# Other start addresses for the split weights, and a strided layout in the first MLP matrix, in a fp32 decoder layer

## The chip, the cores and the metric

The kernel runs on one core of one Trainium2 chip. The metric is the device time of one execution in microseconds (us); lower is better. The times before come from three runs, and one further execution was taken with the hardware profiler.

## What is computed

One layer of a decoder trunk on 512 tokens of width 2048, all in float32. Cut to what matters:

```python
h = rmsnorm(x, g_mix)
z = h @ w_in                                  # 2048 -> 10248 columns
cb, cc, cv, q, k, v, f_logit, gate_c, gate_a = split(z)
conv_branch = (cb * causal_dwconv(cc * cv, conv_w)) @ w_conv_out
attn_branch = forgetting_attention(q, k, v, log_sigmoid(f_logit + b_f)) @ w_attn_out
merged = sigmoid(gate_c + b) * conv_branch + sigmoid(gate_a + b) * attn_branch
x = x + merged @ w_mix_out
h = rmsnorm(x, g_mlp)
u = square(relu(h @ w_ff1))                   # 2048 -> 8192
x = x + u @ w_ff2                             # 8192 -> 2048
return rmsnorm(x, g_final)
```

## The kernel before

Every product of float32 matrices is made of three matmuls in a rounded format (fp32r). Each operand is split into a high part (a rounded copy) and a low part (the rest), and high times high, high times low and low times high are added in PSUM. The helper `split` does this for weights: ScalarE copies the block `src` with rounding into a tile `th` (line 101), and VectorE subtracts that from `src` into a tile `tl` (line 102). `parts` hands out a pair of such tiles from two buffers of each; its argument `at` is the element at which the data begin inside the buffer.

The two large matrices that are multiplied with the normed input, `w_in` and `w_ff1`, go through the class `Group`. A group takes two blocks of columns and both halves of the rows of the weight, and multiplies them by a scheme in the manner of Strassen and Winograd: seven products instead of eight. The seven sums of activation quarters are kept split in the tiles `A11`, `A12`, `A22`, `S1` to `S4`; the sums and differences of weight quarters are made by VectorE in place (line 105, `sub`) in the four load buffers `x0` to `x3`. `head` does the two products `A11` and `A12`, `tail` the other five. Each product is one call of `run`, which asks `parts` for `th` and `tl`, calls `split`, and then calls the group's matmul routine.

- `mm_cols` (lines 136, 138 and 140) is used where the result is wanted with the columns on the partitions: queries and keys (4 groups), the convolution's inputs (6), the gates (8), all from `w_in`, and the whole of `w_ff1` (16 groups). The quarter of the weight is 128 rows by 8 blocks by 256 columns. One stationary operand is 128 columns of one block of `th` or `tl`; the moving operand is 256 tokens of an activation quarter. A run has 48 matmuls: for each of 8 blocks and of 2 halves `j` of the 256 columns one with `th` and the activations' high part (line 136), one with `th` and their low part (138), and then all 16 with `tl` (140). Before, half `j` is 128 neighbouring columns.
- `mm_rows` (lines 154, 156 and 158) has the roles exchanged: the activations are stationary and `th` and `tl` are moving. It is used by the two groups of attention values, `gV1` (260 columns wide) and `gV0` (256), and with 512 columns by the second MLP matrix `w_ff2`, whose seven products are in `unit`.

The constants `WBUF` (2112 elements, the length of one buffer), `SHIFT` and `PAD` (16 elements each) set where data lie. With them every 256-wide group begins 16 elements, 64 bytes, into its buffer; the 260-wide one begins at its start.

Around the change the order is set by the program text: the two products of a head, the attention heads between key/query groups, then the convolution groups, the gates, the branch outputs and `w_mix_out` (`gemm_t` and `gemm_n`, 512 columns, with tiles of their own from `parts`), the first MLP matrix, where the heads of four groups go ahead and the other twelve groups follow whole, and the second. Weights are loaded by SyncE's queue (line 178), one block of 1024 KB each, as soon as one of the four buffers is free. Results of the first MLP matrix are squared, summed and split on ScalarE and VectorE (`put_u`, tiles `r` and `rh`) and written to memory by GpSimd's queue (`s_d`).

Of the kernel before, what the change touches and what calls it, by code (L numbers as in the profile page):

```python
# [15 lines left out]
P = 128  # L16
S = 512
D = 2048
KT = D // P
NT = S // P  # L20
HS = S // 2
# [13 lines left out]
VW = AW // 4  # L35
V1W = (AW // 2 + NH) // 2
QSCALE = float(P) ** -0.5
WBUF, SHIFT, PAD = 33 * 64, 16, 16


ORDER = ("A11", "A12", "S4", "S2", "S3", "S1", "A22")
# [4 lines left out]
def tile_hybrid_block(ctx: ExitStack, tc, x, g_mix, w_in, b_f, b_gate, conv_w, w_conv_out,  # L46
                      w_attn_out, w_mix_out, g_mlp, w_ff1, w_ff2, g_final, out):
    nc = tc.nc
    x, out = x[0], out[0]
    w_in, w_conv_out, w_attn_out, w_mix_out = w_in[0], w_conv_out[0], w_attn_out[0], w_mix_out[0]  # L50
    w_ff1, w_ff2 = w_ff1[0], w_ff2[0]
# [48 lines left out]
    def split(src, hi, lo):  # L100
        nc.scalar.activation(out=hi, in_=src, func=AF.Copy)  # L101
        nc.vector.tensor_tensor(out=lo, in0=src, in1=hi.bitcast(F32), op=ALU.subtract)  # L102

    def sub(out, a, b):
        nc.vector.tensor_tensor(out=out, in0=a, in1=b, op=ALU.subtract)  # L105

    def add(out, a, b):
        nc.vector.tensor_tensor(out=out, in0=a, in1=b, op=ALU.add)  # L108

    def parts(shape, at=0):  # L110

        q, w = shape[1:]
        return tuple(main.tile([P, WBUF], F32R, tag=tag, name=tag, bufs=2)[:, at:at + q * w]
                     .rearrange("p (q c) -> p q c", q=q) for tag in ("th", "tl"))
# [12 lines left out]
    def mm_cols(ps, Sx, hi, lo, first):  # L127

        ps = ps[0].rearrange("p (j s) -> p j s", j=2)
        nq = hi.shape[1]  # L130
        for part in range(2):
            for q in range(nq):
                for j in range(2):
                    o, js = ps[:, j, :], slice(j * P, (j + 1) * P)
                    if part == 0:
                        nc.tensor.matmul(o, hi[:, q, js], Sx[:, 0, q, :], start=first and q == 0 and j == 0, stop=False,  # L136
                                         skip_group_check=True)
                        nc.tensor.matmul(o, hi[:, q, js], Sx[:, 1, q, :], start=False, stop=False, skip_group_check=True)  # L138
                    else:
                        nc.tensor.matmul(o, lo[:, q, js], Sx[:, 0, q, :], start=False, stop=q == nq - 1,  # L140
                                         skip_group_check=True)

    def mm_rows(ps, Sx, hi, lo, first):
# [15 lines left out]
                                         skip_group_check=True)  # L159


    free, later = [0, 1, 2, 3], []

    class Group:

        def __init__(self, view, c1, c2, w, ST, mm, banks, put, scale=1.0):
            self.view, self.cs, self.w, self.ST, self.mm, self.banks = view, (c1, c2), w, ST, mm, banks
            self.put, self.scale, self.at = put, scale, {}  # L170

        def load(self, i, j):

# [8 lines left out]
            return [bank(i, which) for i in self.banks["abcd".index(which)]]  # L182

        def run(self, ps, n, src, first):
            hi, lo = parts([P, KT // 2, self.w], SHIFT if self.w == HS else 0)
            split(src, hi, lo)
            self.mm(ps, self.ST[n], hi, lo, first)

        def snap(self, ps, scale=1.0):
            s = otile([P, 2, self.w], "o")  # L190
# [192 lines left out]
    for t in range(NT):  # L383
        h = xp[t // 2][:, t % 2]
        n = 4 if t == 0 else 2
# [52 lines left out]
    def kq(hp, banks):  # L438
        return Group(w_in, COL_K + hp * HS, COL_Q + hp * HS, HS, Q1.ST, mm_cols, banks, store_kq(hp), QSCALE)
# [16 lines left out]
    def at(name, shape=None, dt=F32):  # L456
        return pb.tile(shape or [P, S], dt, tag="at", name=name, bufs=6)
# [33 lines left out]
    c1 = at("c1", [NH, S])  # L491
# [5 lines left out]
    c2 = at("c2", [NH, S])  # L497
# [80 lines left out]
    n = NH // 2  # L578
    for g in (4, 2, 0, 5, 3, 1):
        def put_z(i, j, v, g=g):  # L580
            f = 4 * (g % 2) + 2 * j
            nc.sync.dma_start(out=z_d[g // 2, f:f + 2, :, i * HS:(i + 1) * HS].rearrange("b p c -> p b c"), in_=v)

        whole(Group(w_in, g * S, g * S + HS, HS, Q1.ST, mm_cols, steady(n), put_z))
        n += 1
        if g < 2:
            for f in range(4 * g, 4 * g + 4):
                conv_job(f)

    for f in range(0, KT, 2):  # L590
        def put_g(i, j, v, f=f):
            for b in range(2):
                k = j * KT + f + b
                nc.scalar.activation(out=v[:, b, :], in_=v[:, b, :], func=AF.Sigmoid, bias=bgT[:, k:k + 1])
            nc.sync.dma_start(out=g_d[j, f:f + 2, :, i * HS:(i + 1) * HS].rearrange("b p c -> p b c"), in_=v)

        whole(Group(w_in, COL_GC + f * P, COL_GA + f * P, HS, Q1.ST, mm_cols, steady(n), put_g))
        n += 1
# [72 lines left out]
    Q2 = Quarters(pc_, gmlpT)  # L671
# [16 lines left out]
    def put_u(g):  # L688
        quarters = {}

        def square(v, out):
            nc.scalar.activation(out=out, in_=v, func=AF.Square)

        def sums(j):
            r = pf.tile([P, 7, HS], F32, tag="r", name="r")
            if j == 0:
                nc.gpsimd.dma_start(out=r[:, 0:6:5], in_=c_d[g])
            else:
                square(quarters[0, j], r[:, 0:6:5])
            low = quarters[1, j]  # L700
            square(low[:, 1, :], r[:, 3, :])
            square(low[:, 0, :], low[:, 0, :])
            add(r[:, 4, :], low[:, 0, :], r[:, 3, :])
            sub(r[:, 1, :], r[:, 0, :], low[:, 0, :])
            sub(r[:, 2, :], r[:, 4, :], r[:, 0, :])
            sub(r[:, 6, :], r[:, 5, :], r[:, 2, :])
            h = pf.tile([P, 7, HS], F32R, tag="rh", name="rh")
            nc.scalar.activation(out=h, in_=r, func=AF.Copy)
            nc.vector.tensor_tensor(out=r, in0=r, in1=h.bitcast(F32), op=ALU.subtract)
            q = 2 * (g % 2) + j  # L710
            nc.gpsimd.dma_start(out=s_d[g // 2][:, :, 0, q, :], in_=h.bitcast(F32))
            nc.gpsimd.dma_start(out=s_d[g // 2][:, :, 1, q, :], in_=r)

        def put(i, j, v):
            nc.scalar.activation(out=v, in_=v, func=AF.Relu)
            if (i, j) == (0, 0):
                square(v, v)
                nc.gpsimd.dma_start(out=c_d[g], in_=v)
                return
            quarters[i, j] = v  # L720
            if j == 0:
                later.append(lambda: sums(0))
            elif len(quarters) == 2:
                sums(1)

        return put

    def ff1(g, banks):
        return Group(w_ff1, g * S, g * S + HS, HS, Q2.ST, mm_cols, banks, put_u(g))

    heads = [ff1(g, ((a,), (3,), (1,), (7,))) for g, a in enumerate((2, 4, 5, 0))]
    for g in heads:
        g.head()
# [6 lines left out]
    for g in range(4, DFF // S):  # L740
        whole(ff1(g, ((2 + 2 * (g % 2),), (3,), (1,), (7,))))
# [15 lines left out]
    def load_sums(seg):  # L757

        ST = {}
        for k, (place, names) in enumerate(((2, ("A11", "S3")), (3, ("S2", "A22")), (5, ("S1", "A12")), (6, ("S4",)))):  # L760
            t = main.tile([P, 2, 2, 4, HS], F32R, tag=f"t{place}", name="us")
            nc.gpsimd.dma_start(out=t[:, :len(names)].bitcast(F32), in_=s_d[seg][:, 2 * k:2 * k + len(names)])
            for e, n in enumerate(names):
                ST[n] = t[:, e]
        return ST
# [12 lines left out]
    def unit(seg, cg, ST):  # L778
# [27 lines left out]
        last = seg == NSEG - 1  # L806
        ends = []
        run(a, "A11", X[0, 0], True)
        sub(X[0, 0], X[0, 1], X[0, 0])
        sub(X[0, 1], X[1, 1], X[0, 1])  # L810
        into(0, 0, a)
        run(d, "S3", X[0, 1], True)
        free.append(at[0, 1])
        t2 = main.tile([P, 4, S], F32, tag="t4", name="t2")
        sub(t2, X[1, 1], X[0, 0])
        into(1, 1, d)
        run(a, "S2", t2, False)
        sub(t2, X[1, 0], t2)
        into(1, 0, a)
# [18 lines left out]
    for seg in range(NSEG):  # L838
# [3 lines left out]
        ST = load_sums(seg)  # L842
# [51 lines left out]
```

## Time and profile before

| | |
|---|---|
| median of 3 runs | 2590.03 us (2586.49 to 2590.83) |
| the profiled execution | 2588.88 us |
| its span, first to last instruction | 2587.2 us |
| mean granted clock of TensorE | 0.989 |
| busy: TensorE matmul | 2488.6 us (96%) |
| busy: TensorE weight load | 2285.7 us (88%) |
| busy: VectorE | 1912.4 us (74%) |
| busy: ScalarE | 1117.6 us (43%) |
| moved by DMA | 475.59 MB, mean 184 GB/s |

PE is TensorE's matmul, PEld its load of a stationary operand, which runs beside it; DVE is VectorE, ACT ScalarE, POOL GpSimd, SP SyncE. A row of a group names line, engine, operation, tiles written and read, shapes and count, then busy time and mean duration in ns, then the idle time before it and what ended that. Matmuls are pipelined: a record of one matmul is longer than the distance to the next, so the pace is read from the distance between starts. A record with "x16" spans sixteen that follow each other, from the start of the first to the end of the last.

### The profile page before, as it was taken

How to read it: one execution, taken by the hardware profiler on the slowest of the kernel's cores; microseconds unless marked ns; L12 is line 12 of the kernel's file. 1: busy time of each engine (PE TensorE's matmuls, PEld its weight loads, DVE VectorE, ACT ScalarE, POOL GpSimd, SP SyncE). 2: the span in 40 equal slices, each digit the busy share in tenths (PEclk: the TensorE clock that was granted, in tenths of full speed). 3: DMA queues.
4: the chain of work that ended last, by engine and by line, in shares of the span. 5: the costliest groups of instructions: out<-in, count | busy, mean ns of one | idle time of the engine just before them, and what ended most of it. 6: DMA issues, size and time to landing. Idle time of an engine off the chain costs nothing. (4 is left out here: it accounts for less than half of the span.)

```text
span 2587.2 us, 39012 instructions
## 1 busy us (share of the span) xinstructions
PE 2488.6 (96%) x16957; PEld 2285.7 (88%) x16957; DVE 1912.4 (74%) x1484; ACT 1117.6 (43%) x1060; POOL 114.6 (4%) x166
## 2 busy tenths in 40 slices
PE   8899999999999999999998999999989999999997
PEld 7889999999999988888998999999987887887875
DVE  7776767869667745325787788887878788788787
ACT  6333333344444622224545566555653333333344
POOL 0000000000000000000001111111110000000000
PEclk9999999999999999999999999999999999999999
DMA  7444444556443544525656756656587565645562
GB/s 238 134 135 153 131 133 134 185 155 203 140 151 116 194 157 142 195 98 197 208 173 216 235 185 207 220 200 227 183 310 269 199 227 211 224 159 185 212 220 90
DMA packets 288223, 475.59 MB, mean 184 GB/s; under 512 B 10076, under 2 KB 196532, under 8 KB 282292
## 3 DMA queue, kind: packets, MB, share of 16 engines
q1 hardware_dynamic: 263936, 340.92, 41.0%
q0 software_dynamic: 23248, 131.08, 13.5%
q8 instruction: 133, 2.18, 0.3%
q10 hardware_dynamic: 868, 1.10, 0.1%
q14 instruction: 38, 0.31, 0.0%
HBM read 376.59 MB, written 96.47 MB: 183 GB/s over the span
## 5 line engine op out<-in xcount | busy, mean ns | idle before, releaser
L102 DVE TENSOR_TENSOR tl<-x,th 128x2048 fp32r<-128x2048 f32 (+1 forms) x252 | 576.2, 2289 | 218.7 <-ACT th L101 195.0
L101 ACT ACTIVATE th<-x 128x2048 fp32r<-128x2048 f32 (+1 forms) x252 | 482.1, 1916 | 552.3 <-PE a L138 213.9
L105 DVE TENSOR_TENSOR x<-x,x 128x2048 f32<-128x2048 f32 (+1 forms) x144 | 329.3, 2287 | 30.0 <-DMA x<-in_w_ff_dram 26.8
L136 PE MATMUL a<-S,th 128*128 128x256 f32 x1088 | 263.2, 284 | 22.1 <-ACT th L101 16.3
L101 ACT ACTIVATE th<-y 128x2048 fp32r<-128x2048 f32 x80 | 153.7, 1921 | 285.5 <-DVE y L105 115.4
L138 PE MATMUL a<-S,th 128*128 128x256 f32 x1088 | 261.3, 283 | 0.0
L136 PEld LDWEIGHTS a<-S,th 128*128 128x128 f32 x1088 | 208.4, 192 | 25.1 <-ACT th L101 18.8
L102 DVE TENSOR_TENSOR tl<-y,th 128x2048 fp32r<-128x2048 f32 x80 | 182.7, 2284 | 44.4 <-ACT th L101 44.4
L154 PE MATMUL a<-th,us 128*128 128x512 f32 x512 | 202.6, 396 | 10.0 <-ACT th L101 8.9
L102 DVE TENSOR_TENSOR tl<-raw,th 128x2048 fp32r<-128x2048 f32 x40 | 91.7, 2292 | 159.4 <-ACT th L101 158.9
L138 PEld LDWEIGHTS a<-S,th 128*128 128x128 f32 x1088 | 208.4, 192 | 0.0
L156 PE MATMUL a<-th,us 128*128 128x512 f32 x512 | 200.5, 392 | 0.0
L101 ACT ACTIVATE th<-raw 128x2048 fp32r<-128x2048 f32 x40 | 76.8, 1919 | 195.3 <-PE pt L293 71.5
L136 PE MATMUL c<-S,th 128*128 128x256 f32 x544 | 134.4, 288 | 10.8 <-ACT th L101 10.8
L140 PE MATMUL a<-S,tl 128*128 128x256 f32 x1088 | 139.2, 279 | 0.0
L158 PE MATMUL a<-tl,us 128*128 128x512 f32 x512 | 137.8, 391 | 1.1 <-DVE tl L102 1.1
L138 PE MATMUL c<-S,th 128*128 128x256 f32 x544 | 133.5, 286 | 0.0
L140 PEld LDWEIGHTS a<-S,tl 128*128 128x128 f32 x1088 | 131.7, 189 | 0.0
L136 PE MATMUL b<-A,th 128*128 128x256 f32 x544 | 129.3, 281 | 2.4 <-ACT th L101 2.4
L154 PEld LDWEIGHTS a<-th,us 128*128 128x128 f32 x512 | 96.9, 189 | 37.0 <-ACT th L101 17.0
L138 PE MATMUL b<-A,th 128*128 128x256 f32 x544 | 128.8, 280 | 0.0
L138 PE MATMUL d<-S,th 128*128 128x256 f32 x544 | 128.5, 280 | 0.0
(221 smaller groups left out, 5865.7 us busy)
## 6 DMA issues: line engine op xcount, KB each, us to landing
x<-in_w_in_dram SPq DMA_DIRECT2D x80, 1024.0 KB, 5.5
x<-in_w_ff_dram SPq DMA_DIRECT2D x72, 1024.0 KB, 7.5
y<-in_w_ff_dram SPq DMA_DIRECT2D x64, 1024.0 KB, 6.1
us<-s_d POOLq DMA_DIRECT2D x24, 2048.0 KB, 9.9
s_d<-rh POOLq DMA_DIRECT2D x32, 896.0 KB, 6.6
s_d<-r POOLq DMA_DIRECT2D x32, 896.0 KB, 8.1
raw<-in_w_mix_out_dram SPq DMA_DIRECT2D x24, 1024.0 KB, 5.0
g_d<-o SPq DMA_DIRECT2D x32, 256.0 KB, 2.1
```

The source lines that it names most:

```text
L101: nc.scalar.activation(out=hi, in_=src, func=AF.Copy)
L102: nc.vector.tensor_tensor(out=lo, in0=src, in1=hi.bitcast(F32), op=ALU.subtract)
L105: nc.vector.tensor_tensor(out=out, in0=a, in1=b, op=ALU.subtract)
L136: nc.tensor.matmul(o, hi[:, q, js], Sx[:, 0, q, :], start=first and q == 0 and j == 0, stop=False, skip_group_check=True)
L138: nc.tensor.matmul(o, hi[:, q, js], Sx[:, 1, q, :], start=False, stop=False, skip_group_check=True)
L140: nc.tensor.matmul(o, lo[:, q, js], Sx[:, 0, q, :], start=False, stop=q == nq - 1, skip_group_check=True)
L154: nc.tensor.matmul(o, Sh[:, q, ts], hi[:, q, :], start=begin and q == 0, stop=False, skip_group_check=True)
L156: nc.tensor.matmul(o, Sl[:, q, ts], hi[:, q, :], start=False, stop=False, skip_group_check=True)
L158: nc.tensor.matmul(o, Sh[:, q, ts], lo[:, q, :], start=False, stop=q == nq - 1, skip_group_check=True)
```

## The change

Two things change, both in where the split weights lie inside their buffers. Each group that uses `mm_cols` gets a number in the order in which groups are made (keys and queries 0 to 3, convolution 4 to 9, gates 10 to 17, first MLP matrix 18 to 33), and its `th` and `tl` begin 4 x (number mod 16) elements, that is a multiple of 16 bytes between 0 and 240, into the buffer, where 64 bytes was the offset of all. The 256-wide group of attention values, which uses `mm_rows`, begins at the buffer's start. Second, with `mixed=True`, which the groups of the first MLP matrix set, the two halves `j` are stored element by element in turn: column c of half j lies at element 2c + j of its row. ScalarE and VectorE write there at a step of 8 bytes, and a matmul's stationary operand is read at a step of 8 bytes. The source is read in the order in which it lay before. The number, order and shape of instructions on every engine stay as they were.

```diff
-WBUF, SHIFT, PAD = 33 * 64, 16, 16
+WBUF, PAD = 33 * 64, 16
...
                 for j in range(2):
-                    o, js = ps[:, j, :], slice(j * P, (j + 1) * P)
+                    o = ps[:, j, :]
                     if part == 0:
-                        nc.tensor.matmul(o, hi[:, q, js], Sx[:, 0, q, :], start=first and q == 0 and j == 0, stop=False,
+                        nc.tensor.matmul(o, hi[:, q, j], Sx[:, 0, q, :], start=first and q == 0 and j == 0, stop=False,
                                          skip_group_check=True)
-                        nc.tensor.matmul(o, hi[:, q, js], Sx[:, 1, q, :], start=False, stop=False, skip_group_check=True)
+                        nc.tensor.matmul(o, hi[:, q, j], Sx[:, 1, q, :], start=False, stop=False, skip_group_check=True)
                     else:
-                        nc.tensor.matmul(o, lo[:, q, js], Sx[:, 0, q, :], start=False, stop=q == nq - 1,
+                        nc.tensor.matmul(o, lo[:, q, j], Sx[:, 0, q, :], start=False, stop=q == nq - 1,
...
-    free, later = [0, 1, 2, 3], []
+    free, later, groups = [0, 1, 2, 3], [], [0]
...
-        def __init__(self, view, c1, c2, w, ST, mm, banks, put, scale=1.0):
+        def __init__(self, view, c1, c2, w, ST, mm, banks, put, scale=1.0, mixed=False):
...
-            self.put, self.scale, self.at = put, scale, {}
+            self.put, self.scale, self.mixed, self.at = put, scale, mixed, {}
+            if mm is mm_cols:
+                self.shift = 4 * (groups[0] % 16)
+                groups[0] += 1
...
         def run(self, ps, n, src, first):
-            hi, lo = parts([P, KT // 2, self.w], SHIFT if self.w == HS else 0)
-            split(src, hi, lo)
-            self.mm(ps, self.ST[n], hi, lo, first)
+            hl = parts([P, KT // 2, self.w], 0 if self.mm is mm_rows else self.shift)
+            if self.mm is mm_cols:
+                src = src.rearrange("p q (j c) -> p q j c", j=2)
+                form = "p q (c j) -> p q j c" if self.mixed else "p q (j c) -> p q j c"
+                hl = tuple(e.rearrange(form, j=2) for e in hl)
+            split(src, *hl)
+            self.mm(ps, self.ST[n], *hl, first)
...
     def ff1(g, banks):
-        return Group(w_ff1, g * S, g * S + HS, HS, Q2.ST, mm_cols, banks, put_u(g))
+        return Group(w_ff1, g * S, g * S + HS, HS, Q2.ST, mm_cols, banks, put_u(g), mixed=True)
```

## The prediction

> **What bounds the kernel now.** I read the page first (busy shares, the chain, the groups), then busy time by stage, then the timeline of TensorE inside stages, then the waits. From the page:
>
> ```profile
> span 2587.2 us, 39012 instructions
> PE 2488.6 (96%) x16957; PEld 2285.7 (88%) x16957; DVE 1912.4 (74%) x1484; ACT 1117.6 (43%) x1060; POOL 114.6 (4%) x166
> PEclk9999999999999999999999999999999999999999
> L102 DVE TENSOR_TENSOR tl<-x,th 128x2048 fp32r<-128x2048 f32 (+1 forms) x252 | 576.2, 2289 | 218.7 <-ACT th L101 195.0
> L101 ACT ACTIVATE th<-x 128x2048 fp32r<-128x2048 f32 (+1 forms) x252 | 482.1, 1916 | 552.3 <-PE a L138 213.9
> L136 PE MATMUL a<-S,th 128*128 128x256 f32 x1088 | 263.2, 284 | 22.1 <-ACT th L101 16.3
> L136 PEld LDWEIGHTS a<-S,th 128*128 128x128 f32 x1088 | 208.4, 192 | 25.1 <-ACT th L101 18.8
> ```
>
> TensorE is occupied for 96% of the span, at full granted clock in nearly every slice. The change touches matmuls of 256 columns (lines 136 to 140) whose stationary operand comes from `th` and `tl`: 34 groups of 7 runs of 48, 11,424 matmuls. How fast do they follow each other? By stage (columns: length, PE busy and count, loads, VectorE, ScalarE, GpSimd, granted clock, DMA):
>
> ```profile
> 410.00:500.00 90.00, 90.00 (x796) 90.00 (x796) 67.85 (x48) 35.66 (x27) 0.30 (x3) 1.00 0.56 178
> 540.00:890.00 350.00, 350.00 (x2974) 350.00 (x2973) 261.08 (x168) 172.03 (x170) 0.30 (x3) 1.00 0.49 154
> 404.00:898.00 494.00, 492.39 (x4216) 492.00 (x4215) 370.53 (x242) 231.01 (x218) 0.70 (x7) 1.00 0.51 162
> 1528.60:1607.70 79.10, 79.10 (x674) 79.10 (x673) 65.99 (x50) 46.46 (x47) 10.08 (x12) 1.00 0.64 213
> 1647.20:1728.10 80.90, 76.75 (x675) 76.36 (x674) 66.94 (x51) 47.08 (x46) 10.11 (x12) 1.00 0.64 214
> 1441.40:1933.50 492.10, 473.44 (x4034) 471.13 (x4032) 406.14 (x302) 282.26 (x276) 64.40 (x79) 0.99 0.64 216
> ```
>
> Two matmuls of each count only overlap the edges. So 90.00/794 = 113.35 ns per matmul in one stretch, 350.00/2972 = 117.77 in another: same shape, same code, same granted clock of 1.00. There are two steady paces, and the timeline shows them inside single runs of 16 `tl` matmuls:
>
> ```profile
> 461.72 1.98 PE L140 MATMUL d<-A,tl 128*128 128x256 f32 x16
> 704.77 2.05 PE L140 MATMUL a<-A,tl 128*128 128x256 f32 x16
> ```
>
> A record spans its first start to its last end, and one matmul takes 0.28, so (1.98 - 0.28)/15 = 113 ns and (2.05 - 0.28)/15 = 118 ns. The slow pace goes on over whole groups without a gap; nothing but the operands' reads is left to differ. Counted by their starts, about 5,700 of the 11,424 go at the slow pace, which is 5,700 x 4.4 ns = 25 us: all that a better placement could return.
>
> Whether a nanosecond per matmul counts differs by stage. From 404 to 898 us (input projection) TensorE is busy 492.39 of 494.00: every nanosecond counts. In the first MLP matrix it is not so: 1528.60 to 1607.70 is two groups at the slow pace (79.10/672 = 117.7 ns) without any idle time, 39.6 us a group; 1647.20 to 1728.10 is two groups at the fast pace, with 4.15 us idle, 40.5 us a group. The faster matmuls made the groups slower. The chain and the waits say why:
>
> ```profile
> 1515.54 1.89 PE d L140 x16
> 1521.19 1.89 PE a L140 x16
> ...
> 1709.73 2.29 DVE tl L102
> 1713.07 2.30 DVE tl L102
> 1715.38 11.65 DMA x<-in_w_ff_dram
> ...
> PE a L136 <- ACT th L101: 12.4, 9, 2.9
> PE a L136 <- ACT o L192: 5.6, 2, 2.8
> PE c L136 <- ACT th L101: 3.3, 1, 3.3
> PE b L136 <- ACT th L101: 2.4, 1, 2.4
> ```
>
> (The last four are TensorE's waits from 1380 to 1935 us: line, releaser, total, times, longest.) At the slow pace the chain runs on TensorE; at the fast pace it leaves it for splits, subtractions and weight loads. The twelve groups from 1441.4 to 1933.5 average 41.0 us, or 122 ns per matmul with its waits.
>
> **The change part by part.** Instructions, order, tiles, waits and transfers stay; only addresses and strides of `th` and `tl` change.
>
> *Starts.* In the built program `th`, `tl` and the activation tiles all begin 192 bytes past a multiple of 256, and rows are 1024 bytes apart. Before, every 256-wide group added 64 bytes; afterwards column group g adds 16 x (g mod 16). Groups 0, 4, 8, 12, ... start on a multiple of 64, the other three in four do not. The trace has no load from such a start. The nearest row has the roles exchanged: the 260-wide values group, whose rows are 1040 bytes apart, so that the moving operand starts at every multiple of 16:
>
> ```profile
> 87.33 1.12 PE L158 MATMUL a<-tl,S 128*128 128x260 f32 x8
> 114.72 1.10 PE L158 MATMUL a<-tl,S 128*128 128x256 f32 x8
> ```
>
> (1.12 - 0.28)/7 = 120 ns for 260 columns, 118.2 scaled to 256; the 256-wide group beside it, at steady 64-byte starts, goes at (1.10 - 0.28)/7 = 117. So mixed starts end at or just above the slow pace, not the fast one. Bounds: 113.35 below (no conflict at all; the gain is then as large as the slow pace's whole cost), 118.2 above; a stationary start could cost more than a moving one, so I keep 120, unscaled, as the far end. I take 118.2, the only measured case of such starts.
>
> Input projection, 404 to 898 us: today (494.0 - 1.6 idle)/4214 = 116.8 ns. 10 of its 13 groups get odd starts: 10 x 336 x (118.2 - 116.8) = +4.7 us. The three key/query groups 1 to 3 before it, between attention heads, get odd starts too. They are mostly at the fast pace:
>
> ```profile
> 280.83 1.98 PE L140 MATMUL a<-A,tl 128*128 128x256 f32 x16
> ```
>
> (the run's last 16, (1.98 - 0.28)/15 = 113 again), so 3 x 336 x (118.2 - 113.4) = +4.8, of which I let a tenth hide in waits on attention: +4.3. Sum +9.0, bounds -15 (all at 113.35) and +17 (all odd ones at 120).
>
> *First MLP matrix, starts.* At 118.2 a group needs 336 x 118.2 = 39.7 us of TensorE, under the present mean of 41.0. The waits named above hide it, as they do in 1528 to 1607. If that cover were gone, the price would be 5,376 x (118.2 - 115.5) = 15 us, 115.5 being the middle of the two paces. I take 0, keeping 12 x (39.7 - 41.0) = -16 (the waits vanish as they did there) and +15.
>
> *First MLP matrix, stride.* A load now takes every second element: 128 values 8 bytes apart, 1024 bytes instead of 512. No load of the trace does that. How much slack has a load? A load and a matmul of only 128 columns:
>
> ```profile
> 27.32 1.95 PE L355 MATMUL ptr<-dg,xn 128*128 128x128 f32 x16
> 242.28 0.38 PE L539 MATMUL tp<-ident,p 128*128 128x128 f32 x2
> ```
>
> (1.95 - 0.30)/15 = 110 ns, 0.38 - 0.27 = 110 ns. The matmul side of 128 columns would be about half of 113, so 110 is probably the load's own floor: it lies 3 ns under the matmul. A strided load 3% slower becomes the bound, and one 11% slower (122 ns) uses up the cover of the waits. Bounds: nothing, and a load that takes twice as long, 220 ns: 5,376 x (220 - 122) = +527 us. I take nothing, since the matmul's own moving operand covers 1024 bytes in 113 ns (the row at 461.72), which is what the strided load now has to do.
>
> *Writes of the splits.* ScalarE and VectorE now write `th` and `tl` 8 bytes apart over three dimensions. Splitting a pattern into blocks costs nothing already:
>
> ```profile
> L102 DVE TENSOR_TENSOR A<-h,A 128x1024 fp32r<-128x1024 f32 x12 | 14.3, 1218 | 0.8 <-ACT A L101 0.8
> ```
>
> 1218 for 1024 in eight blocks is 74 ns more than half of the 2289 for 2048 in one, so blocks cost next to nothing. Element stride on the write is not in the trace. Taken at 0; far end, a write at half rate: +2.29 us in each of 7 `tl` per group. VectorE is busy 406.14 of 492.10, 33.8 us a group; 49.8 would bound it: 16 x 8.8 = +141 us.
>
> Sum: 9.0 + 0 + 0 + 0 = +9. The profiled execution took 2588.88 (1.7 beyond its span), the median is 2590.03, the runs go from 2586.49 to 2590.83. 2588.9 + 9.1 = **2598**. A measurement of this kernel tells about 0.2% (5 us) from no change.
>
> The Trainium skill, "SBUF — State Buffer", section "Specifications (TRN2)", says that SBUF has 16-byte lines and that two hits per line give full bandwidth. By that both halves of the change are free, since every start is a line's start and stride 2 leaves two fp32 per line, and the sum would be 0. The 260-wide row does not agree for starts: they too begin on lines.
>
> **The rivals.**
> *Faster.* The two paces are a phase between the streams that matmul and load read; a group with a new offset breaks a slow one, and at stride 2 both streams walk 1024 bytes per period, so they never overtake each other. For: identical addresses give both paces, and a pace changes only after a gap. Against: odd starts are slow in the only place that has them. Input projection at 113.35: 4,214 x 3.5 = -14.7 us; the MLP gains nothing, its fast groups need 40.5. 2574.
>
> *Slower, by the strided load.* It decides from 122 ns on, per nanosecond 5.4 us. At 136 ns (a fifth slower) TensorE needs 45.7 us a group: 16 x 4.7 + 9 = +84, 2673; doubled, 3125. For: 3 ns of slack. Against: nothing measured.
>
> *Slower, by strided writes.* It decides once VectorE has over 41.0 us a group, that is from (41.0 - 33.8)/7 = 1.0 us more per `tl`; at half rate 2739. For and against: no row has such a write.
>
> *Nothing happens.* Placement is not what sets the pace, but when the last gap ended; the slow share stays. 2589. By the Trainium skill's rule on lines it comes out here too.
>
> **How the numbers follow.** Forecast 0.44 (its own range 2590 to 2612), faster 0.30, strided load 0.11, strided writes 0.05, nothing 0.10. The range goes down to 2570 for the faster rival, and up to 2650, where the strided load is 16% slower; the rest of the two slow rivals, some 0.12, and a few hundredths below are left out. Slower: 0.38 of the forecast and 0.16 = 0.54; same: 0.10 and 0.05 of the forecast = 0.15; faster: 0.31.
>
> **What would show it.** Pace by group in 404 to 898 us: 118 in odd-start groups makes the first step right; 113 throughout makes the faster rival right; above 120 makes my bound wrong. In the MLP, `x16` records of line 140's successor: up to 122 ns without a longer group confirms the cover; above, with no idle PE, the strided load. ScalarE's 1916 and VectorE's 2289 ns for `th` and `tl` must stay. A group in the MLP under 39 us, or changes in a stage with no 256-column matmuls, would be outside all of this.

## The result, and the profile after

| | before | after |
|---|---|---|
| median of 3 runs | 2590.03 us | 2610.72 us (2606.12 to 2611.18) |
| the profiled execution | 2588.88 us | 2611.18 us |
| its span | 2587.2 us | 2609.5 us |

The change made the kernel slower: the ratio of the times, after to before, is 1.0078, 95% interval 1.0055 to 1.0101. 2598 was forecast; 2610.72 lies inside the range, 12.7 us above the forecast value. The page of the kernel after, in the same rows as shown of before:

```profile
span 2609.5 us, 39012 instructions
PE 2524.7 (97%) x16957; PEld 2323.0 (89%) x16957; DVE 1912.0 (73%) x1484; ACT 1140.7 (44%) x1060; POOL 114.6 (4%) x166
PEclk9999999999999999999999999999999999999999
L102 DVE TENSOR_TENSOR tl<-x,th 128x2048 fp32r<-128x2048 f32 (+1 forms) x252 | 576.3, 2289 | 243.2 <-ACT th L101 219.3
L101 ACT ACTIVATE th<-x 128x2048 fp32r<-128x2048 f32 (+1 forms) x252 | 504.9, 2007 | 559.4 <-PE a L138 220.7
L136 PE MATMUL a<-S,th 128*128 128x256 f32 x1088 | 267.1, 285 | 16.3 <-ACT th L101 10.8
```

The counts are the same. TensorE is busy for 36.1 us more, ScalarE for 23.1 us more (the mean of a `th` rises from 1916 to 2007 ns), VectorE for the same time. Busy time by stage, for the input projection from its second convolution group to its last gate (13 groups; the first convolution group is interleaved with the last attention heads and is left out), and for the twelve whole groups of the first MLP matrix (columns: window, length, PE, PEld, VectorE, ScalarE and GpSimd busy with counts, granted clock, DMA share, GB/s). Before, whose second stage is the last row of the prediction's table of stages:

```profile
387.40:898.70 511.30, 509.69 (x4369) 509.30 (x4368) 385.69 (x251) 238.19 (x223) 0.70 (x7) 1.00 0.50 159
```

After:

```profile
395.40:914.00 518.60, 518.60 (x4371) 518.60 (x4370) 385.80 (x251) 240.58 (x223) 0.70 (x7) 1.00 0.50 156
1458.00:1958.60 500.60, 488.18 (x4033) 486.37 (x4031) 405.24 (x302) 297.20 (x276) 64.38 (x79) 1.00 0.64 213
```

The profiled executions differ by 22.3 us of span. Following the same instructions through both, in order: the first 256-column matmul of a column group starts 4.0 us later (56.2 for 52.2 us), the stretch from there to the second convolution group (attention values, keys and queries, attention heads, first convolution group) takes 339.2 for 335.2 us (+4.0), the next, the 13 groups above, 518.5 for 511.3 (+7.2), the first MLP matrix from its first head to its last group 688.3 for 678.2 (+10.1), what lies between -0.1, the rest -2.9 us.

Of the first 4.0 us 3.8 come ahead of everything that the change touches: the first matmul of the 256-wide values group, the earliest one with moved operands, starts at 44.7 us, for 40.9 before. The same two kernels over the first 52 us, before and then after:

```profile
0.00:52.00 52.00, 40.16 (x319) 39.30 (x320) 37.74 (x62) 30.76 (x50) 3.32 (x13) 1.00 0.78 252
```

```profile
0.00:52.00 52.00, 38.81 (x287) 37.96 (x288) 33.94 (x61) 27.99 (x48) 3.32 (x13) 1.00 0.73 234
```

TensorE has begun 32 instructions fewer, with less moved by DMA (234 for 252 GB/s). Nothing changed ahead of that group, and over the profiled kernels of this study the first 256-column matmul of a column group starts at 51.8 to 56.2 us; I count this as difference between executions.

Now the pace of matmuls in single groups of the kernel after (columns: window, length, PE busy and count, granted clock, DMA). The windows lie in the groups that begin 128 and 224 bytes into their buffers:

```profile
525.00:555.00 30.00, 30.00 (x252) 1.00 0.51 158
765.00:795.00 30.00, 30.00 (x259) 1.00 0.51 158
```

Without the two records that overlap the edges: 120.0 and 116.7 ns, without idle time, at full granted clock. From group 5 on, each group of this profile keeps its pace from its first run to its last. The distances between starts of matmuls, averaged over runs without waits, give this table (ns; "contiguous" is `w_in` after the change, and where a second value stands it or the first is from the kernel with the starts alone or from the first runs of the scan, both below; "interleaved" is `w_ff1` after the change, stride 2):

| begins at, bytes | 0 | 16 | 32 | 48 | 64 | 80 | 96 | 112 |
|---|---|---|---|---|---|---|---|---|
| contiguous | 120.0 | 118.3 | 118.4 | 117.8 or 123.0 | 113.3 or 117.8 | 118.7 | 118.7 or 120.1 | 120.0 |
| interleaved | 120.0 | 120.0 | 120.0 | 121.4 | 120.1 | 117.8 | 120.7 | 120.0 |

| begins at, bytes | 128 | 144 | 160 | 176 | 192 | 208 | 224 | 240 |
|---|---|---|---|---|---|---|---|---|
| contiguous | 118.7 or 120.0 | 118.3 or 120.0 | 119.9 | 118.1 | 117.8 | 116.7 or 120.0 | 116.7 or 117.8 | 117.4 or 119.9 |
| interleaved | 121.0 | 118.8 | 120.0 | 122.2 | 121.6 | 118.7 | 120.0 | 118.4 |

The 64 bytes of before are the only contiguous start that has the pace of 113.3 ns. In the MLP, TensorE's waits after the change, from 1390 to 1960 us (the view of the prediction's last rows: line, releaser, total, times, longest):

```profile
PE a L136 <- ACT th L101: 7.5, 7, 2.2
PE c L136 <- ACT th L101: 7.4, 2, 3.8
PE a L136 <- ACT o L199: 5.5, 3, 3.7
PE b L136 <- ACT th L101: 1.0, 1, 1.0
```

They did not vanish, although the matmuls are slower: these four come to 21.4 us, the prediction's four, over 1380 to 1935 us, to 23.7.

### The profile page after: what moved, and what is told of

Same layout as the page of the kernel before. It is cut to its first block, busy times and chain, and to the rows that moved or that the text cites. A ratio compares the mean times of both kernels' runs of the same rounds, so it can differ in the third digit from the quotient of the medians.

```text
span 2609.5 us, 39012 instructions
## 1 busy us (share of the span) xinstructions
PE 2524.7 (97%) x16957; PEld 2323.0 (89%) x16957; DVE 1912.0 (73%) x1484; ACT 1140.7 (44%) x1060; POOL 114.6 (4%) x166
## 5 line engine op out<-in xcount | busy, mean ns | idle before, releaser
L101 ACT ACTIVATE th<-x 128x2048 fp32r<-128x2048 f32 (+1 forms) x252 | 504.9, 2007 | 559.4 <-PE a L138 220.7
L136 PE MATMUL a<-S,th 128*128 128x256 f32 x1088 | 267.1, 285 | 16.3 <-ACT th L101 10.8
L138 PE MATMUL a<-S,th 128*128 128x256 f32 x1088 | 265.6, 284 | 0.0
L136 PEld LDWEIGHTS a<-S,th 128*128 128x128 f32 x1088 | 210.2, 193 | 18.7 <-ACT th L101 12.6
L136 PE MATMUL b<-A,th 128*128 128x256 f32 x544 | 131.9, 283 | 1.0 <-ACT th L101 1.0
L138 PE MATMUL d<-S,th 128*128 128x256 f32 x544 | 132.0, 283 | 0.0
L136 PE MATMUL d<-S,th 128*128 128x256 f32 x544 | 131.6, 282 | 0.0
L138 PE MATMUL a<-A,th 128*128 128x256 f32 x544 | 131.6, 283 | 0.0
```

The lines of the kernel that those rows point to most:

```text
L136: nc.tensor.matmul(o, hi[:, q, j], Sx[:, 0, q, :], start=first and q == 0 and j == 0, stop=False, skip_group_check=True)
L138: nc.tensor.matmul(o, hi[:, q, j], Sx[:, 1, q, :], start=False, stop=False, skip_group_check=True)
```

## Experiments

Ratios are of times to the kernel before on the same chip, with 95% intervals. The theory: the distance between the starts of the stationary and the moving operand, modulo 256 bytes, sets the pace. In every 256-column matmul the activations begin 192 bytes past a multiple of 256, and so does the buffer of the weight part; the offset inside the buffer is therefore this distance. Rivals: the stationary operand's own place sets it; or the stride, or ScalarE's slower split, and not the starts.

**The parts of the change, one at a time.** First the starts alone, without interleaving:

```diff
-        return Group(w_ff1, g * S, g * S + HS, HS, Q2.ST, mm_cols, banks, put_u(g), mixed=True)
+        return Group(w_ff1, g * S, g * S + HS, HS, Q2.ST, mm_cols, banks, put_u(g))
```

> The 16 starts kept, every group contiguous (the interleaving in the first MLP matrix is undone). Theory A (each start has a pace of its own, set by where the stationary block starts against the moving one): 404 to 898 us of before stays as in the changed kernel, 116.7 to 120.0 ns per matmul by start, about +11 us; in the MLP each start repeats the pace that it had in the input projection (for instance 113.3 or 117.8 at 64 bytes, 120.0 at 0 and 128), ScalarE's th back at 1916 ns, and the MLP within 4 us of before, so about 2601. Rival B (the odd paces come from gaps and have nothing to do with the start): paces of 113.3 and 117.8 only, 2585 to 2595. Rival C (starts cost in the MLP too, cover gone): +7 more, 2608.

Median 2604.2 us, ratio 1.0078 (1.0055 to 1.0100): the same as the whole change. The stages of its profiled execution:

```profile
391.60:910.20 518.60, 518.60 (x4370) 518.60 (x4369) 385.44 (x251) 240.46 (x223) 0.70 (x7) 1.00 0.50 156
1454.80:1949.00 494.20, 484.62 (x4034) 482.87 (x4032) 405.20 (x302) 283.11 (x276) 64.35 (x79) 0.99 0.64 216
```

The input projection takes 518.60 us, as after the change, but not at the same paces. The groups at 128 and at 144 bytes, in this kernel:

```profile
513.00:550.00 37.00, 37.00 (x314) 1.00 0.43 136
553.00:590.00 37.00, 37.00 (x311) 1.00 0.45 133
```

By the starts they go at 118.7 and 120.0 ns, where the kernel after has 120.0 and 118.3, each constant over the group, with the same addresses, in the same order and without idle time in either. So 64 bytes is not the only start with two paces, and that the two stretches agree to 0.1 us is in part chance, because the two differences cancel. In the MLP four more starts (48, 208, 224 and 240 bytes) show a second pace, so the expectation that each start repeats its pace there did not hold; the time of the MLP's whole groups was within 4 us of before, as it said (494.20 for 492.10).

Then interleaving alone, all column groups at 64 bytes as before:

```diff
-                self.shift = 4 * (groups[0] % 16)
+                self.shift = 16
...
-            hl = parts([P, KT // 2, self.w], 0 if self.mm is mm_rows else self.shift)
+            hl = parts([P, KT // 2, self.w], (16 if self.w == HS else 0) if self.mm is mm_rows else self.shift)
```

> Starts of before (64 bytes in every 256-wide group), the interleaving of the first MLP matrix kept. Theory A: the input projection goes back to before (113.3 and 117.8 ns), the MLP has 120.1 ns in every run as the changed kernel had at this start, ScalarE's th at 2116 ns; MLP +5 to +8 us, total 2594 to 2598. Rival C (the stride costs nothing, the starts did it all): 2586 to 2592.

Median 2591.62 us, ratio 1.0020 (0.9996 to 1.0043). Its stages, the MLP's whole groups and a stretch of the input projection:

```profile
1429.80:1925.00 495.20, 487.66 (x4034) 1.00 0.64 215
540.00:850.00 310.00, 310.00 (x2736) 1.00 0.50 156
```

In the MLP every run goes at 120.0 ns (by starts); before it was 113.3 or 117.8. So the strided load does cost 2 to 7 ns a matmul at this start, and yet the time hardly moves: it misses the 2594 to 2598 of the theory and lies in the range of rival C. The pace of 120.0 is a single one, with none of the two that the contiguous load has at 64 bytes. In the same execution the input projection goes at 310.00/2734 = 113.4 ns from beginning to end, where before had a mixture; nothing was changed there.

Interleaving has two sides, the strided write of the splits and the strided load. In the next two kernels only one is strided, so the columns of the first MLP matrix come out permuted inside their groups.

```diff
                 form = "p q (c j) -> p q j c" if self.mixed else "p q (j c) -> p q j c"
-                hl = tuple(e.rearrange(form, j=2) for e in hl)
-            split(src, *hl)
+                wr = tuple(e.rearrange(form, j=2) for e in hl)
+                hl = tuple(e.rearrange("p q (j c) -> p q j c", j=2) for e in hl)
+            split(src, *wr)
```

> As stride_only, but the matmuls read their stationary columns contiguously: the columns of the first MLP matrix come out permuted, the work is the same. It has the strided writes of ScalarE and VectorE without the strided loads. Theory A: th 2116 ns, tl 2289, matmuls at 113.3 or 117.8 ns; if the longer th is what the MLP loses, +5 to +7 us (2595 to 2597), if the loads are what it loses, 2588 to 2592.

> As stride_only, but the splits write contiguously and the matmuls read every second element: columns permuted again, the work is the same. Strided loads without strided writes. Theory A: th 1916 ns, matmuls at 120.1 ns; if the loads are what the MLP loses, +5 to +7 us (2595 to 2597); if the waits cover them as the prediction had it, 2586 to 2592. Rival: both halves together are needed, and each alone is within 2 us of before.

(The kernel with the load alone has `wr` contiguous and `hl` interleaved.) Strided write: 2590.24 us, ratio 1.0018 (0.9990 to 1.0045). Strided load: 2583.5 us, ratio 0.9983 (0.9958 to 1.0008). The page's row of ScalarE's splits, of the strided write, then of the strided load:

```profile
L101 ACT ACTIVATE th<-x 128x2048 fp32r<-128x2048 f32 (+1 forms) x252 | 502.7, 1998 | 542.4 <-PE a L138 208.9
```

```profile
L101 ACT ACTIVATE th<-x 128x2048 fp32r<-128x2048 f32 (+1 forms) x252 | 482.5, 1917 | 571.5 <-PE a L138 232.9
```

The slower ScalarE is the write's. Neither half costs anything that can be told: the 2595 to 2597 us that either theory had for a half that carries the loss came in neither. And the MLP's whole groups (window, length, PE busy and count), strided write, then strided load:

```profile
1451.70:1948.80 497.10, 470.58 (x4034) 0.99 0.65 216
```

```profile
1449.00:1938.40 489.40, 486.92 (x4034) 1.00 0.64 216
```

With the strided load alone TensorE is busy 13.5 us longer than before (486.92 for 473.44) and the groups are not slower: 489.40 for 492.10 us, with idle time down to 2.5 us. That is the cover by waits of which the prediction spoke, at its fullest. With ScalarE's slower split alone the idle time is 26.5 us, for 18.7 before. Both are differences of single profiled executions, and this stage varies by 13 us between executions that have the same instructions there (see below).

**The distance or the place.** All starts at 0, and then both operands moved, the weights to 128 bytes and the activations by 64, so that their distance is 64 bytes as before:

```diff
-                self.shift = 4 * (groups[0] % 16)
+                self.shift = 0
```

> Contiguous everywhere, all groups begin at the buffer's start, so stationary and moving operand start alike modulo 256 bytes, both on a multiple of 64. Theory A (the distance of the two starts sets the pace): 120.0 ns in every run of every group, no fast pace anywhere; input projection 404 to 898 us of before +13, key/query groups +5; MLP covered up to 2 us; about +18, 2606. Rival B (what costs is a start off a multiple of 64 bytes): 113.3 or 117.8 as before, 2580 to 2595.

```diff
-WBUF, SHIFT, PAD = 33 * 64, 16, 16
+WBUF, SHIFT, PAD = 33 * 64, 32, 16
...
     main.tile([P, PAD], F32, tag="pad", name="lay")
+    main.tile([P, PAD], F32, tag="pad2", name="lay")
```

(the second diff is against the kernel before)

> Contiguous everywhere; a pad of 64 bytes moves the activation tiles, and all 256-wide groups begin 128 bytes into the buffer. The distance between the starts is 64 bytes as before, but both starts are 64 bytes further on. Theory A (distance): only 113.3 and 117.8 ns as before, 2570 to 2601. Rival D (the stationary operand's own place modulo 256): 120.0 ns, which 64 bytes modulo 256 had in the changed kernel, about 2606.

At 0: 2613.02 us, ratio 1.0100 (1.0048 to 1.0153). Both moved: 2599.96 us, ratio 1.0081 (1.0052 to 1.0110). Inside the input projection, at 0 and then both moved:

```profile
540.00:890.00 350.00, 350.00 (x2919) 1.00 0.48 150
```

```profile
540.00:890.00 350.00, 349.90 (x3084) 1.00 0.51 161
```

350.00/2917 = 120.0 ns at a distance of 0, and no other pace in any group; 113.5 ns in the other, whose stationary operand begins where the 128-byte one of the kernel after begins, which went at 120.0 (118.7 with the starts alone). In the MLP the other has both 113.3 and 117.8 ns, the two paces of before. So the place of the stationary operand alone does not set the pace, and the distance fits all of it; only one distance was tested in this way, with one shift of 64 bytes. That the kernel with both moved is slower all the same comes from the stages with 512 columns, where the extra 64 bytes changed a distance too. The second MLP matrix after the change, where the distance is that of before, then with both moved:

```profile
2100.00:2300.00 200.00, 198.38 (x863) 1.00 0.61 216
```

```profile
2100.00:2300.00 200.00, 199.67 (x847) 1.00 0.56 193
```

198.38/861 = 230 ns, 199.67/845 = 236 ns for 512 columns, waits and missing records included; the distances between starts, over the whole stage, average 227 and 233 ns. From its first matmul to its last the stage takes 647.7 us, for 633.1 before (+14.6), and what lies between the last gate and the first MLP matrix 362.8 for 356.0 (+6.8). Together that is about the 0.81% of the ratio.

**Which of the two paces.** At 64 bytes there are two. Here the first run of each group of the input projection begins elsewhere (a different offset in each of fourteen groups), the six others at 64 bytes:

```diff
-            self.run(self.a, "A11", X[0, 0], True)
+            first = SHIFT
+            if self.mm is mm_cols and self.view is w_in:
+                if seen[0] >= 4:
+                    first = SCAN[seen[0] - 4]
+                seen[0] += 1
+            self.run(self.a, "A11", X[0, 0], True, first)
```

> Before, with one difference: in 14 groups of the input projection (the last six of the convolution and the gates, 404 to 898 us and the group before) the first of the seven runs begins at another start, a different one in each group; the six runs behind it at 64 bytes as before, with no gap between. Theory A: that first run has the pace its start had in the changed kernel; the pace of the six behind it (113.3 or 117.8) is set by what came directly before them, so it can differ from group to group, and the same starts give the same pace in another execution. Rival E (the pace at 64 bytes changes only at a gap): all 14 groups have one pace behind the first run, as before.

Median 2583.47 us, ratio 0.9990 (0.9967 to 1.0014). The six runs behind the first of three successive groups, whose first run began at 160, 176 and 192 bytes:

```profile
705.00:737.00 32.00, 32.00 (x285) 1.00 0.47 141
743.00:776.00 33.00, 33.00 (x283) 1.00 0.45 140
783.00:815.00 32.00, 32.00 (x285) 1.00 0.48 142
```

113, 117.4 and 113 ns; by the starts 113.33, 117.77, 113.33, each constant over six runs. TensorE was idle in none of the three. So a pace is changed by a run at another start as well, without a gap, and with the same addresses afterwards. The six runs went at 117.8 behind first runs at 16, 32 and 176 bytes, at 113.3 behind ten others; the group with 0 was disturbed by waits. The first run itself cost least, 116.6 ns, at 208 and 224. One part of the expectation failed: first runs at 96, 128 and 144 bytes went at 120.1, 118.6 and 119.8 ns, where the kernel after has 118.7, 120.0 and 118.3, so a first run did not always have the pace of its start in the changed kernel.

**A version with the first runs moved.** Against the kernel before:

```diff
+RESET = 52
...
-            self.run(self.a, "A11", X[0, 0], True)
+            first = RESET if self.mm is mm_cols and self.view is w_in else SHIFT
+            self.run(self.a, "A11", X[0, 0], True, first)
```

> The kernel before, but in every 256-wide group of w_in with mm_cols (4 of keys and queries, 6 of the convolution, 8 gates) the first of the seven runs begins 208 bytes into its buffers; the other six, and the first MLP matrix, stay at 64. Theory (the distance between the operands' starts sets the pace; at 64 bytes there are two, and which one is taken up depends on the start just before): after a run at 208 bytes the six go at 113.3 ns in every group, as in the scan, so the input projection from the first convolution group to the last gate takes 495 to 497 us in every execution (before: 496 or 514 by chance), the spread of the executions shrinks, and the median is 2570 to 2580, ratio 0.993 to 0.998. Rival (the pace is taken up by chance at each group, and the scan's pattern was luck): some groups go at 117.8 again, median as before within 0.3%.

> As the kernel whose first runs begin at 208 bytes, but these begin at 32 bytes. Theory: the scan showed 117.8 ns after that start, so the six other runs of every group in the input projection go at 117.8, it takes 513 to 516 us, and the median is 2590 to 2600, 15 to 20 us above the kernel with 208. Rival (chance): the two kernels have the same median within 0.3%, and both show a mixture of the paces.

> As the kernel whose first runs begin at 208 bytes, with the same first run in the 16 groups of the first MLP matrix as well. Theory: these go at 113.3 ns too, but there the waits on splits and weights fill the time (40.5 us a group at the fast pace before, 39.6 to 41 at the slow one), so the whole is the same as with the reset in w_in alone within 4 us. Rival (each nanosecond of the pace counts there as in w_in): 16 x 336 x 2 to 4 ns, that is 11 to 23 us less than with the reset in w_in alone.

208 bytes: 2575.82 us, ratio 0.994 (0.992 to 0.996), runs from 2565.54 to 2577.75. 32 bytes: 2587.92, ratio 1.0003 (0.9978 to 1.0029), runs from 2573.89 to 2599.24. 208 bytes in the MLP too: 2576.16, ratio 0.995 (0.9929 to 0.9971): nothing more than in `w_in` alone, so the reset pays only where TensorE doesn't wait. (In its profile most runs of the MLP do go at 113.3 ns, but behind a wait some groups take up 117.8 until the next first run.) The expectation for 32 bytes failed: in the profile the six runs go at 113.3, not 117.8, and the executions scatter as those of before. The input projection with 208, and with 32:

```profile
540.00:890.00 350.00, 350.00 (x3071) 1.00 0.51 161
```

```profile
540.00:890.00 350.00, 349.99 (x3069) 1.00 0.51 162
```

In the scan the start at 32 bytes had come behind a group that was slow already. So I took it for a start that leaves the pace as it is, and tried the one that had turned a fast pace slow, 176 bytes, beside a second run of 208, on another chip:

> As the kernel whose first runs in w_in begin at 208 bytes, but these begin at 176 bytes. In the scan that start turned the 113.3 ns of the group before into 117.8, without a gap; the start at 32 bytes came there after a group that was already at 117.8, and in the profile with resets at 32 bytes the pace stayed at 113.3. So the new theory has three kinds of start: some that set the fast pace, some that set the slow one, some that leave the pace as it is. By it 176 bytes gives 117.8 ns in the six other runs of every group from the first convolution group to the last gate: 13 x 288 x 4.4 = 16.6 us more than with 208, that stretch 514 to 517 us, median 2590 to 2598, few executions below 2585. Rival (a start never sets the slow pace for certain, only the fast one): mixture, spread from 2573 to 2600 as before, median within 0.3% of before.

> The same kernel as the one with first runs at 208 bytes, once more beside the one with 176. Theory: again 113.3 ns in the six other runs of every group from the first convolution group on, median 2570 to 2580, ratio 0.992 to 0.997, highest execution under 2583. Rival (the first result was luck): as before, 2588 with a spread of 25 us.

176 bytes: 2587.84 us (2580.32 to 2591.64), ratio 1.002 (0.9995 to 1.0044). 208 bytes again: 2576.9 us (2570.15 to 2581.75), ratio 0.9984 (0.9962 to 1.0005). The two lie 11 us apart and their runs hardly overlap. But 176 is no sure way to the slow pace. Two successive groups of its profile:

```profile
437.00:469.00 32.00, 32.00 (x274) 1.00 0.47 145
476.00:508.00 32.00, 32.00 (x285) 1.00 0.78 246
```

117.6 and 113 ns. Of the thirteen groups eight went at 117.8, four at 113.3, and one changed in its middle, at a wait. Both of its expectations, slow in all, or chance with the spread of before, are too simple. The pace ahead of the first run matters too: by the starts, each of the eight groups of this profile that came behind 113.3 ns, three of them ahead of the thirteen, took up 117.8; behind 117.8 the thirteen kept it and left it in turn, so that slow, slow, fast repeats as long as no wait comes between.

With 208 bytes the six runs went at 113.3 in every group from the second convolution group on, in both profiles, as in the scan. That alone shows little, because in 25 of these 26 groups the pace was 113.3 already; the profile with 32 bytes has the same picture. What shows the effect are the places where 117.8 went ahead: there are three in these two profiles and six in the one with the MLP's first runs moved too, and behind each of these nine first runs, without idle time, the next run goes at 113.3, from its third matmul at the latest. One of the six, the runs ahead of such a first run in the MLP (window, length, PE busy and count, granted clock, DMA) and those behind it:

```profile
1581.00:1603.00 22.00, 22.00 (x189) 1.00 0.89 297
1609.50:1628.00 18.50, 18.50 (x166) 1.00 0.51 157
```

117.6 and 113 ns. The executions agree with it: none of the 18 with 208 bytes took over 2582 us, while before reaches 2598 and 2595 on the two chips. On the first chip it is faster than the kernel before by 0.6%; on the second it is not told apart from it, because before was faster there itself (2579.22, runs from 2568.7 to 2595.19); the expected ratio of 0.992 to 0.997 was missed. Its own medians agree within 1.1 us, and its spread is 12 us where before has 27. The kernel after was not run beside it; by the ratios to before on each chip (0.994 and 0.9984 against 1.0078) it is 0.9 to 1.4% faster than that.

## Why the prediction was right or wrong

**Which stage counts: right.** In the input projection each nanosecond reached the time: 509.69/4367 = 116.7 ns before, 518.60/4369 = 118.7 after, 518.60 again with the starts alone. In the MLP much of it did not.

**Starts in the input projection: right in sign and near in size, with the wrong rule and some luck.** +4.7 was forecast, +7.2 came. The mean of the ten groups with odd starts is 118.6, close to the 118.2 taken from the 260-wide group, but they lie between 116.7 and 120.0: one row cannot stand for all starts. The rule behind the step, that starts off a multiple of 64 cost and the others stay at the 116.8 of before, is wrong: those at 0 and 128 bytes went at 120.0, the one at 192 at 117.8, while 208 and 224 bytes cost less than the slow pace. What the runs fit is the distance to the moving operand, and of all starts only 64 bytes has the fast pace. The size depends also on the mixture of paces in the one profiled execution of before: with the same addresses this stage took 495.7 us in the kernel with interleaving alone and 514.3 with the strided write alone or the strided load alone (first to last start; before 511.4, after 518.4). Against these the same change would have shown 4 to 23 us. The prediction had seen the two paces, but not that the mixture differs so much from one execution to the next.

By the rule of the Trainium skill ("SBUF — State Buffer", "Specifications (TRN2)"), as the prediction read it, all starts on a 16-byte line should cost the same. These runs do not agree: 113.3 to 123.0 ns, all on such lines.

**Keys and queries: the sum agrees by luck.** +4.3 was forecast for groups 1 to 3, and their stretch shows +4.0. But groups 1 to 3 themselves take 167.3 us for 165.7, +1.6, and four profiles with the addresses of before in them go from 165.7 to 167.3. Waits between the attention heads hide most of the slower pace, not the tenth that was allowed. The rest of the +4.0 is in the stretch of group 0 (116.3 for 113.6 us), which begins at 0 bytes and goes at 119.9 for 113.3 ns, and of the 256-wide values group (119.9 for 117.8), for which the forecast had no term.

**The first MLP matrix: taken as 0, and open.** 0 was taken; the profiled executions differ by 10.1 us there, 8.5 of them in the twelve whole groups. TensorE was busy 14.7 us longer (488.18 for 473.44), and the idle time gave back only 6.2 (12.4 for 18.7). The prediction let the waits hide everything up to 122 ns. They hid 13.5 us in the kernel with the strided load alone, and less here. ScalarE's slower split comes at the same time here, and from 1390 to 1960 us TensorE still waited 15.9 us for `th` (18.1 before), but that the two together are the reason is not shown. Nor is it shown how much of the 8.5 us the change itself causes: the same stage, with the same addresses and instructions as before, took 487.8 to 500.9 us in six profiles (the kernel before, the scan, and the four with first runs moved in `w_in` alone), and 500.6 after is inside that range.

**Strided load: right in the time, wrong in the reason.** The term was put at nothing because a load of 1024 bytes should fit into the 113 ns that the moving operand takes. It did not: 120.0 ns at the start where the contiguous load has 113.3 or 117.8, and up to 122.2 with other starts. Whether the load is then the bound, or the two reads hinder each other, no run tells apart. The cover by waits is what held: the 122 from which it was to decide was just reached, and alone it cost nothing that could be measured (0.9958 to 1.0008).

**Strided write: wrong for one engine, without effect by itself.** Both means were to stay. ScalarE's and VectorE's splits in the MLP's whole groups, before and then after:

```profile
L102 DVE TENSOR_TENSOR tl<-x,th 128x2048 fp32r<-128x2048 f32 x83 | 189.9, 2288 | 51.5 <-ACT th L101 51.5
L101 ACT ACTIVATE th<-x 128x2048 fp32r<-128x2048 f32 x83 | 158.6, 1912 | 108.1 <-DVE x L105 46.9 <-PE a L138 45.2 <-PE d L138 6.3
```

```profile
L102 DVE TENSOR_TENSOR tl<-x,th 128x2048 fp32r<-128x2048 f32 x83 | 190.0, 2290 | 61.8 <-ACT th L101 61.7
L101 ACT ACTIVATE th<-x 128x2048 fp32r<-128x2048 f32 x83 | 175.6, 2118 | 112.5 <-PE a L138 47.1 <-DVE x L105 46.9 <-PE d L138 9.1
```

ScalarE takes 206 ns more for 2048 elements, VectorE 2 ns. The step had bounded only VectorE's; the price fell on the engine that had time to spare, 297 of 500 us busy, and alone it changed the time by -0.10% to +0.45%.

**The rivals.** "Faster" was right that the two paces belong to one set of addresses, and wrong that a new offset or stride 2 would lead to the fast one. Its argument that a pace changes only after a gap holds while the start stays (in the input projection before changes once, in a gap) and fails where the start changes, as the scan shows. Its other idea, that one run at a new offset breaks a slow pace, came true in the kernel with first runs at 208 bytes. That history decides between the paces of one distance fits its phase between two streams of reads; no run shows the phase itself. "Nothing" fell with the starts alone: 1.0055 at the least.

**The sum.** +9.0 was forecast. +22.3 in the profiled spans are +11.2 from the two stages of that forecast, +10.1 in the MLP, +4.0 ahead of the change, -0.1 and -2.9. By the ratios, starts alone and the whole change are the same 0.8%, and each half of the interleaving lies around zero; so the starts carry the loss, and what interleaving adds to them is too small to be told. That 2610.72 lies in the range rests on the width of the range as much as on the sum: of the forecast's +9.0, the input projection is borne out, the keys and queries are not, and 0.8%, some 20 us, is twice what was forecast. Where the other half arises with the starts alone stays open; the mixture of paces in the unprofiled executions of before is not on record.

## What to carry to other kernels

Where TensorE never waits, lay both operands' starts out together: the distance between them went with the pace here, 113.3 to 120.0 ns in the input projection, 6%, and a pad in front of one tile cost some 21 us in stages that nobody had meant to touch. A kernel whose executions scatter by 1% at a full granted clock may have two paces for one layout; read the distance between starts of matmuls group by group, in more than one profile, before believing a gain or a loss of that size. One profile of the changed kernel made most starts look as if they had a single pace; the second profile, with the same addresses, showed otherwise. And before the difference of two profiles in a stage is called an effect, look how far that stage differs between profiles that have the same instructions there: it was 13 us in the first MLP matrix.

## What the runs showed of the hardware that was not expected

- With 256 columns, stationary and moving operand 64 bytes apart, fp32r matmuls kept either 113.3 or 117.8 ns for hundreds of microseconds at a granted clock of 1.00. Other distances have two paces too: 118.7 or 120.0 ns at 128 bytes and 118.3 or 120.0 at 144, each kept over a whole group with the same addresses. At a distance of 0 all 34 groups went at 120.0.
- 48 matmuls with another start in between can change the one pace into the other without idle time: 208 bytes turned 117.8 into 113.3 in nine of nine cases. 176 bytes turned 113.3 into 117.8 in eight of eight groups of one profile, and behind 117.8 led to either, in turn. Why stays open.
- With 512 columns a distance of 64 bytes was slower than a distance of 0: 233 ns, for 227.
- ScalarE wrote 2048 values 8 bytes apart in 2118 ns, for 1912 side by side; VectorE's time stayed at 2290.
- With a stationary operand read at a step of 8 bytes the matmuls went at 117.8 to 122.2 ns, by start. A load twice as long, the far end of the prediction, did not occur.
